# Up projection by seven block products per pair of inner tiles, with token-block sums made beside two plain pairs

## Chip, cores and metric

One core of one Trainium2 chip runs the whole layer. The metric is the device time of one execution in microseconds, median of several runs; the profile is one execution taken by the hardware profiler. Its span is the time from the first to the last instruction.

## What is computed

A decoder layer with 1024 tokens, width 1024 and 4096 inner channels, float32. The part that matters here is the feed-forward block at its end:

```python
x = x + jnp.concatenate([attn, conv], axis=-1) @ w_out[l]
h = rmsnorm(x, norm_ffn_g[l])
x = x + jnp.square(jax.nn.relu(h @ w_ffn_up[l])) @ w_ffn_down[l]
return rmsnorm(x, norm_final_g)
```

`h @ w_ffn_up` is 1024x1024 by 1024x4096, `... @ w_ffn_down` 1024x4096 by 4096x1024.

## The kernel before

Every float32 product is made of three reduced-precision matmuls: `split` (lines 54 to 56) makes a rounded high part on ScalarE and the remainder on VectorE or GpSimd (POOL), and `mm3` (lines 58 to 61) issues high x high, high x low and low x high into one PSUM bank.

The stages that the change and the prediction speak of, in order:

- **Output projection, convolution half, and the second norm** (lines 842 to 849). For each of 8 token tiles t, `conv_proj` makes 2 x 12 matmuls (tile `oc`) that VectorE adds to the residual `x2[t]`; `norm_rows` squares the row sum on ScalarE (line 116), takes the root on POOL (lines 82, 83) and scales on VectorE (line 145, tile `n_xn`, two buffers); `norm_cols` transposes on TensorE (line 151) and splits the result into `h2h`, `h2l`, which hold the normed tokens as [channel, token], one tile for each half of 512 tokens.
- **Up projection** (lines 871 to 894, 957 to 965), 16 pairs of inner tiles of 128 channels. `load_up` loads one pair of 1 MB a pair ahead and splits it. `up` makes four results of 128 channels by 512 tokens, each 8 x 3 matmuls: 96 matmuls a pair. ScalarE makes the relu (line 880), VectorE the product with it (line 881), then four sums (lines 889 to 892), and SP stores seven tiles of 256 KB to DRAM (`hid`). Those sums are what the down projection needs.
- **Down projection** (lines 897 to 1026). It already works by seven block products for eight, in 7 groups of 7 steps of 24 matmuls; an eighth group is plain. `prep` splits the operands two steps ahead, three buffers of `hi` and `lo`; `load_group` loads the next group; `sums` makes the weight differences on POOL. Of the seven sums of results, three lie in `xe` and four in the residual tiles `x2a`, to which VectorE adds (line 993). Tokens 0 to 511 and 512 to 1023 are the two token blocks; even and odd inner tiles, and the two halves of the output width, are the other blocks.
- **The end** (lines 1028 to 1057): the eighth group, the residual, the last norm and the store.

The order on each engine, the DMA queue SP among them, is set at build time by a scheduler with a timing model of its own (line 1085); each engine then runs its instructions strictly in that order, waiting on semaphores. A pool opened where another was released waits only for the tiles whose place it takes (`reuse_waits="tile"`). DMAs are all issued by SP; a DMA also waits for the landing of the one eight places before it.

Of the kernel before, what the change touches and what calls it, by code (L numbers as in the profile page):

```python
# [33 lines left out]
def body(tc, x, norm_mix_g, w_in, b_forget, conv_dw_w, conv_dw_b, conv_ln_g, conv_ln_b,  # L34
# [830 lines left out]
    def raw4(name):  # L865
        return rp.tile([P, 2, HN], F32, tag="raw4", name=name, bufs=11)
# [4 lines left out]
    def up(p, w):  # L871
        q = [raw4(f"q{p}{e}") for e in range(2)]
        for e in range(2):
            sl = slice(e * P, (e + 1) * P)
            for hf in range(2):
                ps = ps_two(f"up{p}{e}{hf}")[:, 0, :]
                for k in range(KT):
                    mm3(ps, w[0][:, k, sl], w[1][:, k, sl], h2h[hf][:, k, :], h2l[hf][:, k, :], k == 0, k == KT - 1)
                r = rp.tile([P, HN], F32, tag="r", name=f"r{p}{e}{hf}", bufs=2)
                A.activation(r, ps, AF.Relu)  # L880
                V.tensor_tensor(q[e][:, hf, :], ps, r, op=ALU.mult)  # L881
        a11, a21, a12, a22 = q[0][:, 0, :], q[0][:, 1, :], q[1][:, 0, :], q[1][:, 1, :]
        if p >= NPAIR - 2:
            for i, a in ((1, a11), (2, a12), (0, a21), (4, a22)):
                SP.dma_start(hid[i][p if i else p - NPAIR + 2], a)
            return
        s12, s34 = raw4(f"s12{p}"), raw4(f"s34{p}")
        s1, s2, s3, s4 = s12[:, 0, :], s12[:, 1, :], s34[:, 0, :], s34[:, 1, :]
        V.tensor_tensor(s1, a21, a22, op=ALU.add)
        V.tensor_tensor(s2, s1, a11, op=ALU.subtract)  # L890
        V.tensor_tensor(s3, a11, a21, op=ALU.subtract)
        V.tensor_tensor(s4, a12, s2, op=ALU.subtract)
        for i, a in ((1, a11), (2, a12), (4, a22), (5, s1), (6, s2), (7, s3), (3, s4)):
            SP.dma_start(hid[i][p], a)
# [9 lines left out]
    def wtile(g, name, dt=F32):  # L904
        if g == 0:
# [183 lines left out]
```

## Time and profile before

| what | before |
|---|---|
| median of 3 runs (lowest to highest) | 1196.79 us (1196.76 to 1197.3) |
| the profiled execution's own time | 1197.22 us |
| its span | 1195.2 us |
| granted TensorE clock, mean over the span | 0.995 |
| TensorE (PE) busy | 1158.0 us, 97% |
| VectorE (DVE) busy | 770.7 us, 64% |
| ScalarE (ACT) busy | 442.2 us, 37% |
| POOL busy | 330.0 us, 28% |
| DMA | 145.63 MB, mean 122 GB/s |

PE is the matrix engine, PEld its weight loads, which run beside it. Busy time is the union of an engine's instructions; L59 is line 59 of the kernel. An idle time is followed by what ended it in brackets. Consecutive matmuls overlap, so their spacing is read from start times, not from their durations.

### The profile page before, as it was taken

Reading aid. Unit: us, or ns where it says so; the run is one execution under the profiler, and the core shown is the slowest. Engines: PE = TensorE matmul, PEld = TensorE weight load, DVE = VectorE, ACT = ScalarE, POOL = GpSimd, SP = SyncE. Lnnn points to the kernel's source line nnn. Section 1 sums busy time; section 2 is a strip of 40 time slices with the busy share of each in tenths; the row PEclk is TensorE's granted clock in tenths of the full one; section 3 lists DMA queues with packets and bytes.
Section 4 is the critical chain, followed back from the end, with each engine's and each line's share of the span. In section 5 each row is a group of like instructions: output and inputs, shape, how many; then the busy total and the mean of one; then the engine's idle time right before and its main releaser. Section 6 shows DMA issues by size and latency. Waiting matters only on the chain.

```text
span 1195.2 us, 14915 instructions
## 1 busy us (share of the span) xinstructions
PE 1158.0 (97%) x5623; PEld 948.2 (79%) x5623; DVE 770.7 (64%) x1026; ACT 442.2 (37%) x691; POOL 330.0 (28%) x272
## 2 busy tenths in 40 slices
PE   6999999989999999979999999999999999999997
PEld 6899888767677688868888888888888888888876
DVE  5399999568888764552332423423268888878994
ACT  6322452147888841331211212111235343433422
POOL 7113255037788610100000000000163334443011
PEclk9999999999999999989999999999999999999999
DMA  8021045774232253023343443532495554444003
GB/s 267 13 60 49 23 122 126 205 192 123 72 116 62 84 179 91 1 80 103 118 167 106 138 144 107 172 111 104 159 347 189 168 164 137 136 154 141 1 12 129
DMA packets 92912, 145.63 MB, mean 122 GB/s; under 512 B 7896, under 2 KB 43048, under 8 KB 92840
## 3 DMA queue, kind: packets, MB, share of 16 engines
q1 hardware_dynamic: 92840, 144.68, 38.4%
q8 instruction: 44, 0.72, 0.2%
q14 instruction: 28, 0.23, 0.1%
HBM read 104.18 MB, written 40.40 MB: 121 GB/s over the span
## 4 chain that ended last, share of the span: by engine, by line
PE 86%; DVE 6%; issue 3%; ACT 2%; POOL 2%; DMA 1%; SPq 0%; DVEq 0%; POOLq 0%; ACTq 0%
PE up L60 10%; PE up L59 10%; PE up L61 10%; PE dn L61 7%; PE dn L59 7%; PE dn L60 7%; PE qk L59 2%; PE qk L60 2%; PE qk L61 2%; PE g L269 2%; PE v L61 1%; PE v L60 1%; PE v L59 1%; PE oc L59 1%; PE oc L60 1%
## 5 line engine op out<-in xcount | busy, mean ns | idle before, releaser
L881 DVE TENSOR_TENSOR q<-up,r 128x512 f32<-128x512 f32 x64 | 44.1, 689 | 161.4 <-ACT r L880 161.4
L292 DVE SCALAR_TENSOR_TENSOR conv<-u,par,conv 128x1024 f32<-128x1024 f32 x108 | 133.6, 1279 | 1.7 <-ACT conv L287 1.3
L880 ACT ACTIVATE r<-up 128x512 f32<-128x512 f32 x64 | 37.9, 593 | 216.3 <-PE up L61 216.3
L56 POOL TENSOR_TENSOR d01lo<-b,d01hi 128x1024 fp32r<-128x1024 f32 x1 | 2.4, 2392 | 326.6 <-ACT d01hi L55 326.6
L993 DVE TENSOR_TENSOR x<-dn,x 128x1024 f32<-128x1024 f32 x56 | 67.9, 1218 | 25.1 <-PE dn L61 25.0
L56 POOL TENSOR_TENSOR pl<-pt,ph 128x512 fp32r<-128x512 f32 (+3 forms) x71 | 74.7, 1067 | 26.2 <-ACT ph L55 22.4
L613 ACT ACTIVATE pt<-sT,ctok 128x512 f32<-128x512 f32 (+1 forms) x96 | 54.4, 585 | 11.6 <-PE sT L611 5.1
L453 DVE CUSTOM_DVE_ANT_0 mj<-s,ck 128x512 bf16<-128x512 f32 (+2 forms) x64 | 37.4, 584 | 19.5 <-PE s L447 13.5
L55 ACT ACTIVATE ph<-pt 128x512 fp32r<-128x512 f32 (+1 forms) x96 | 48.7, 530 | 0.6
L993 DVE TENSOR_TENSOR xe<-dn,xe 128x1024 f32<-128x1024 f32 x36 | 42.8, 1212 | 4.0 <-PE dn L61 4.0
L59 PE MATMUL qk<-hTh,wh_qk 128*128 128x512 f32 x96 | 39.0, 406 | 0.0
L60 PE MATMUL qk<-hTl,wh_qk 128*128 128x512 f32 x96 | 37.9, 395 | 0.0
L445 PE MATMUL s<-ks,q 128*128 128x512 f32 (+2 forms) x96 | 36.8, 390 | 1.0 <-DVE m L453 0.9
L61 PE MATMUL qk<-hTh,wl_qk 128*128 128x512 f32 x96 | 37.8, 394 | 0.0
L633 PE MATMUL av<-pl,v 128*65 128x512 f32 (+1 forms) x96 | 32.7, 341 | 3.9 <-POOL pl L56 2.3
L61 PE MATMUL v<-wh_v,hTl 128*128 128x260 f32 x128 | 36.2, 282 | 0.0
L60 PE MATMUL v<-wl_v,hTh 128*128 128x260 f32 x128 | 36.1, 282 | 0.0
L59 PE MATMUL v<-wh_v,hTh 128*128 128x260 f32 x128 | 36.0, 281 | 0.0
L631 PE MATMUL av<-ph,v 128*65 128x512 f32 (+1 forms) x96 | 35.5, 370 | 0.2 <-ACT ph L55 0.2
L608 PE MATMUL sT<-q,ks 128*128 128x512 f32 (+1 forms) x96 | 34.1, 355 | 0.1
L609 PE MATMUL sT<-qx,kx 66*128 66x512 f32 (+3 forms) x96 | 33.7, 351 | 0.0
L82 POOL TENSOR_SCALAR rs_tmp<-n_ss 128x1 f32<-128x1 f32 x16 | 6.6, 414 | 96.5 <-ACT n_xn L116 80.6
(926 smaller groups left out, 3692.2 us busy)
## 6 DMA issues: line engine op xcount, KB each, us to landing
h<-hid SPq DMA_DIRECT2D x53, 512.0 KB
b<-in_w_ffn_down SPq DMA_DIRECT2D x32, 512.0 KB
hid<-s SPq DMA_DIRECT2D x56, 256.0 KB
hid<-q SPq DMA_DIRECT2D x50, 256.0 KB
xp<-in_x SPq DMA_DIRECT2D x8, 512.0 KB
qstack<-qk SPq DMA_DIRECT2D x32, 128.0 KB
kstack<-qk SPq DMA_DIRECT2D x32, 128.0 KB
ks<-kstack SPq DMA_DIRECT2D x8, 512.0 KB
```

Of the source, the lines that this page charges most:

```text
L55: A.activation(hi, src, AF.Copy)
L56: eng.tensor_tensor(lo, src, f32(hi), op=ALU.subtract)
L59: T.matmul(ps, sh, mh, start=first, stop=False)
L60: T.matmul(ps, sh, ml, start=False, stop=False)
L61: T.matmul(ps, sl, mh, start=False, stop=last)
L292: V.scalar_tensor_tensor(dst, u[:, k:k + S], tap_w(c, k), cell[0], op0=ALU.mult, op1=ALU.add)
L445: T.matmul(ps[:, :w], d["q2"][:, i * P:(i + 1) * P], d["ks"][:, b0:b1], start=True, stop=b1 < n)
L453: V.tensor_tensor_reduce(junk[:, :w], ps[:, :w], d["ck"][:, b0:b1], op0=ALU.subtract, op1=ALU.max, scale=1.0, scalar=d.pop("m0") if b0 els ...
L613: A.activation(pt[:, :w], ps[:, :w], AF.Exp, bias=ctok[:, h * NT + kt:h * NT + kt + 1])
L880: A.activation(r, ps, AF.Relu)
L881: V.tensor_tensor(q[e][:, hf, :], ps, r, op=ALU.mult)
L993: V.tensor_tensor(a, ps, a, op=ALU.add)
```

## The change

In 14 of 16 pairs (pairs 2 to 15) the four results of a pair come from seven block products of 4 x 3 matmuls each, 84 matmuls in place of 96. The blocks are the two halves of the 1024 input channels, the two inner tiles of the pair, and the two token blocks. For this

- each pair's weights are loaded as four blocks of 256 KB, four sums or differences are made of them on POOL, and seven blocks (in place of eight) are split;
- of the tokens, four sums or differences of blocks (`mov[5]`, `mov[6]`, `mov[4]` and `mov[7]`) are made once, beside pairs 0 and 1, which stay plain. Their unsplit source is a float32 copy of the transposed normed tokens that `norm_cols2` writes to DRAM (`hraw`), tile by tile, and that is read back;
- after the products, results are combined: two ScalarE copies, one POOL add, six VectorE operations that read PSUM, and the square of the relu as one more VectorE operation on each of four results;
- for room, the residual goes to DRAM (`x2d`) and comes back at the start of the down projection into tiles that the up projection uses meanwhile; `raw4` has 8 buffers for 11 and its pool opens in the middle of the last pair, when products 1, 5 and 6 of it are made; the raw weights have 3 buffers for 2;
- the first two results of pair 0, on the first token block, are made ahead of the last tile's norm.

The core of the diff:

```diff
+    def norm_cols2(t):
...
+        split(h2h[hf][:, :, c:c + P], h2l[hf][:, :, c:c + P], pt.rearrange("p (k n) -> p k n", k=KT))
+        A.activation(xn, pt, AF.Copy)
+        SP.dma_start(hraw[:, :, t * P:(t + 1) * P].rearrange("k p n -> p k n"), xn.rearrange("p (k n) -> p k n", k=KT))
+    for t in range(NT):
+        for hf in range(2):
+            conv_proj(hf, t)
+        SP.dma_start(x2d[t], x2[t])
+        xns[t] = norm_rows(x2[t], gffn, pn, f"n2_{t}")
         if t >= 1:
-            norm_cols(xns.pop(t - 1), t - 1, h2h, h2l, f"n2_{t - 1}")
+            norm_cols2(t - 1)
...
+    def load_up7(p):
...
+        for dst, k0, e in ((g[2][:, 0], 0, 1), (g[2][:, 1], 4, 1), (g[0][:, 0], 0, 0), (g[1][:, 1], 4, 0)):
+            SP.dma_start(dst, w_up_k[:, k0:k0 + 4, c0 + e * P:c0 + (e + 1) * P])
+        G.tensor_tensor(g[0][:, 1], g[2][:, 0], g[2][:, 1], op=ALU.add)
+        G.tensor_tensor(g[1][:, 0], g[0][:, 1], g[0][:, 0], op=ALU.subtract)
+        G.tensor_tensor(g[2][:, 0], g[0][:, 0], g[2][:, 0], op=ALU.subtract)
+        split(ah[:, 0:2], al[:, 0:2], g[0])
+        split(ah[:, 2:4], al[:, 2:4], g[1])
+        G.tensor_tensor(g[1][:, 1], g[1][:, 1], g[1][:, 0], op=ALU.subtract)
+        split(bh[:, 0], bl[:, 0], g[1][:, 1])
+        split(bh[:, 1:3], bl[:, 1:3], g[2])
...
+    def make_moving(k):
+        b11, b12, b22, b21 = [load_hraw(f"b{r}{c}_{k}", 4 * r + k, c) for r, c in ((0, 0), (0, 1), (1, 1), (1, 0))]
+        G.tensor_tensor(b11, b12, b11, op=ALU.subtract)
+        split(*mov[5][k], b11)
+        G.tensor_tensor(b22, b22, b11, op=ALU.subtract)
+        split(*mov[6][k], b22)
+        G.tensor_tensor(b21, b21, b22, op=ALU.subtract)
+        split(*mov[4][k], b21)
+    def make_t3(k):
+        b12, b22 = load_hraw(f"c12_{k}", k, 1), load_hraw(f"c22_{k}", 4 + k, 1)
+        G.tensor_tensor(b12, b22, b12, op=ALU.subtract)
+        split(*mov[7][k], b12)
...
+    def up7(p, w, mid=None):
...
+        def relu2(dst, ps, other):
+            V.tensor_tensor(dst, ps, other, op=ALU.add)
+            V.scalar_tensor_tensor(dst, dst, 0.0, dst, op0=ALU.max, op1=ALU.mult)
+        A.activation(s1, prod(p, w, 1), AF.Copy)
+        A.activation(s5, prod(p, w, 5), AF.Copy)
+        V.tensor_tensor(u2, prod(p, w, 6), s1, op=ALU.add)
+        if mid is not None:
+            mid()
+        G.tensor_tensor(s5, s5, u2, op=ALU.add)
+        relu2(q[:, 0, 0, :], prod(p, w, 2), s1)
+        relu2(q[:, 0, 1, :], prod(p, w, 3), s5)
+        p7 = prod(p, w, 7)
+        V.tensor_tensor(u2, p7, u2, op=ALU.add)
+        relu2(q[:, 1, 1, :], p7, s5)
+        sums_up(p, False)
+        relu2(q[:, 1, 0, :], prod(p, w, 4), u2)
+        sums_up(p, True)
...
+    for e in range(2):
+        up_half(0, uws[0], e, 0, ps_mm(f"up0{e}0"))
+    norm_cols2(NT - 1)
...
+            load_h(0, SEQ0[3])
+            reload_x2(0)
+            reload_x2(1)
+            load_h(0, SEQ0[4])
+            reload_x2(2)
+            reload_x2(3)
+            for i in SEQ0[5:]:
                 load_h(0, i)
             sums(0)
-            V.tensor_tensor(acc_of[3], acc_of[3], acc_of[5], op=ALU.subtract)
             continue
         g, i = steps[n]
+        if n == 3:
+            for h in range(2):
+                V.tensor_tensor(acc_of(3, h), acc_of(3, h), acc_of(5, h), op=ALU.subtract)
```

What the scheduler makes of it, at three places. **ScalarE at the end of the second norm**, tiles 5 to 7 (`n_7_t` the transposed tile 7, `n_7_xn` its normed rows; `work_q<-up` the relu of pair 0). Before:

```order
L55 ACTIVATE h2h_5103<-n_4_t 128x8x128
L116 ACTIVATE n_6_xn,n_6_ss<-x_4822 128x1024
L55 ACTIVATE up2h<-up2r_5517 128x1024
L55 ACTIVATE up2h<-up2r_5521 128x1024
L55 ACTIVATE h2h_5103<-n_5_t 128x8x128
L55 ACTIVATE h2h_5103<-n_6_t 128x8x128
L55 ACTIVATE up4h<-up4r_5654 128x1024
L116 ACTIVATE n_7_xn,n_7_ss<-x_4822 128x1024
L55 ACTIVATE up4h<-up4r_5658 128x1024
L55 ACTIVATE h2h_5103<-n_7_t 128x8x128
```

With the change:

```order
L55 ACTIVATE uhi2a<-ur_5711 128x1024
L854 ACTIVATE n_4_xn<-n_4_t 128x1024
L55 ACTIVATE uhi2a<-ur_5712 128x1024
L55 ACTIVATE h2h_5106<-n_5_t 128x8x128
L889 ACTIVATE work_q<-up_5523 128x512
L116 ACTIVATE n_6_xn,n_6_ss<-x_4825 128x1024
L854 ACTIVATE n_5_xn<-n_5_t 128x1024
L889 ACTIVATE work_q<-up_5550 128x512
L116 ACTIVATE n_7_xn,n_7_ss<-x_4825 128x1024
L55 ACTIVATE h2h_5106<-n_6_t 128x8x128
L854 ACTIVATE n_6_xn<-n_6_t 128x1024
L55 ACTIVATE h2h_5106<-n_7_t 128x8x128
```

The square of tile 6 (L116) moved behind a copy of tile 4 into its old buffer (L854), the split of tile 6 behind the square of tile 7; on PE the transposes of tiles 6 and 7 stand after all 48 early matmuls of pair 0.

**ScalarE at the start of the down projection** (`d05hi` is the split of step 5 of group 0: `h` its tokens, `t` or `b` its weights). Before:

```order
L991 ACTIVATE xe<-dn_7755 128x1024
L991 ACTIVATE xe<-dn_7769 128x1024
L55 ACTIVATE d05hi<-h_0_7713 128x1024
L55 ACTIVATE d05hi<-t_0_7721 128x1024
L55 ACTIVATE d06hi<-h_0_7715 128x1024
L55 ACTIVATE d06hi<-t_0_7722 128x1024
L55 ACTIVATE d07hi<-h_0_7717 128x1024
```

With the change:

```order
L1136 ACTIVATE xe<-dn_7945 128x1024
L1136 ACTIVATE xe<-dn_7959 128x1024
L55 ACTIVATE d05hi<-h_0_7892 128x1024
L55 ACTIVATE d06hi<-h_0_7900 128x1024
L55 ACTIVATE d07hi<-h_0_7908 128x1024
L55 ACTIVATE d05hi<-t_0_7912 128x1024
L55 ACTIVATE d06hi<-t_0_7913 128x1024
```

The weight half of step 5 moved behind the token halves of steps 6 and 7; there are three `hi` buffers, so `d07hi` takes the place of `d03hi`.

**POOL beside pairs 0 and 1** (`b_0` to `b_3` and `c_0` to `c_3`: token blocks read back; `ur`: weights of pair 3). Before, POOL has nothing between the last norm and the first split of the down projection. With the change:

```order
L965 TENSOR_TENSOR b_2_5734<-b_2_5736,b_2_5734 128x512
L930 TENSOR_TENSOR ur_5887<-ur_5889 128x512
L967 TENSOR_TENSOR b_2_5738<-b_2_5738,b_2_5734 128x512
L931 TENSOR_TENSOR ur_5888<-ur_5887 128x512
L932 TENSOR_TENSOR ur_5889<-ur_5887,ur_5889 128x512
L965 TENSOR_TENSOR b_3_5751<-b_3_5753,b_3_5751 128x512
L969 TENSOR_TENSOR b_2_5740<-b_2_5740,b_2_5738 128x512
L967 TENSOR_TENSOR b_3_5755<-b_3_5755,b_3_5751 128x512
L969 TENSOR_TENSOR b_3_5757<-b_3_5757,b_3_5755 128x512
L974 TENSOR_TENSOR c_0_5910<-c_0_5912,c_0_5910 128x512
```

Ahead of these stand six more for `b_0` and `b_1`, behind them three for `c_1` to `c_3`: 19 new operations between the norm and the end of pair 1.

## Rows read from the trace of the kernel before

**Rows 1.** Busy time of the page, engines' share of the span.

```profile
PE 1158.0 (97%) x5623; PEld 948.2 (79%) x5623; DVE 770.7 (64%) x1026; ACT 442.2 (37%) x691; POOL 330.0 (28%) x272
```

**Rows 2.** Windows: stretch, length, busy time (count) by engine, PEclk, DMA share, GB/s.

```profile
510.00:520.00 10.00, 6.49 (x37) 5.28 (x35) 8.00 (x8) 6.06 (x7) 0.74 (x2) 1.00 0.33 102
520.00:526.00 6.00, 1.50 (x7) 1.53 (x8) 4.77 (x4) 2.08 (x4) 1.73 (x2) 0.55 0.30 92
548.00:570.00 22.00, 22.00 (x99) 18.22 (x98) 7.53 (x10) 4.29 (x6) 0.00 (x0) 1.00 0.39 133
885.00:890.00 5.00, 5.00 (x24) 4.14 (x23) 5.00 (x3) 2.01 (x2) 4.92 (x3) 1.00 1.05 401
1100.00:1150.00 50.00, 49.45 (x215) 39.64 (x214) 48.39 (x42) 18.32 (x19) 4.79 (x2) 1.00 0.01 4
```

**Rows 3.** Instructions of tiles up and dn: ns min/median/max, first and last start.

```profile
L59 PE MATMUL up<-h2h,up0h x32: 387/389/776, 526.1 to 547.9; 128*128 128x512 f32 x32
L59 PEld LDWEIGHTS up<-h2h,up2h x32: 187/188/188, 548.4 to 569.4; 128*128 128x128 f32 x32
L59 PE MATMUL up<-h2h,up2h x32: 389/389/390, 548.6 to 569.7; 128*128 128x512 f32 x32
L59 PE MATMUL up<-h2h,up4h x32: 389/389/390, 570.3 to 591.4; 128*128 128x512 f32 x32
L59 PE MATMUL dn<-d01hi x8: 389/389/390, 875.0 to 879.7; 128*128 128x512 f32 x8
```

**Rows 4.** PE in order of time, last two transposes of the norm.

```profile
515.46 1.03 PE L151 MATMUL n_t<-ident,n_xn 128*128 128x128 f32 x8
524.50 1.94 PE L151 MATMUL n_t<-ident,n_xn 128*128 128x128 f32 x8 [8.01 <-DVE n_xn L145]
```

**Rows 5.** ScalarE, POOL and VectorE in order of time, one tile's norm.

```profile
484.55 1.06 ACT L116 ACTIVATE n_xn<-x 128x1024 f32<-128x1024 f32 x1 [1.89 <-DVE x L815]
487.17 1.03 ACT L55 ACTIVATE h2h<-n_t 128x1024 fp32r<-128x1024 f32 x1 [1.47 <-PE n_t L151]
...
485.78 0.19 POOL L82 TENSOR_SCALAR rs_tmp<-n_ss 128x1 f32<-128x1 f32 x1 [5.96 <-ACT n_xn L116]
486.06 0.55 POOL L83 TENSOR_TENSOR n_rs<-rs_tmp,mhalf 128x1 f32<-128x1 f32 x1
...
486.90 1.28 DVE L145 SCALAR_TENSOR_TENSOR n_xn<-x,n_rs,gffn 128x1024 f32<-128x1024 f32 x1
488.22 1.22 DVE L56 TENSOR_TENSOR h2l<-n_t,h2h 128x1024 fp32r<-128x1024 f32 x1
```

**Rows 6.** SP and ScalarE in order of time: one 512 KB load and its reader.

```profile
851.35 0.46 SPq L920 DMA_DIRECT2D h<-hid  x1
...
855.34 1.06 ACT L55 ACTIVATE d02hi<-h 128x1024 fp32r<-128x1024 f32 x1 [0.37 <-DMA h<-hid]
```

**Rows 7.** Groups by form: count, busy us, mean ns, idle before.

```profile
L881 DVE TENSOR_TENSOR q<-up,r 128x512 f32<-128x512 f32 x64 | 44.1, 689 | 161.4 <-ACT r L880 161.4
L889 DVE TENSOR_TENSOR s<-q,q 128x512 f32<-128x512 f32 x14 | 9.7, 692 | 0.5
L56 DVE TENSOR_TENSOR up8l<-up8r,up8h 128x1024 fp32r<-128x1024 f32 x2 | 2.4, 1222 | 5.0 <-ACT up8h L55 5.0
L880 ACT ACTIVATE r<-up 128x512 f32<-128x512 f32 x64 | 37.9, 593 | 216.3 <-PE up L61 216.3
L55 ACT ACTIVATE up6h<-up6r 128x1024 fp32r<-128x1024 f32 x2 | 2.0, 1052 | 4.6 <-PE up L60 4.6
L936 POOL TENSOR_TENSOR t<-b,b 128x1024 f32<-128x1024 f32 x7 | 17.9, 2552 | 32.5 <-issue 12.9 <-DMA b<-in_w_ffn_down 5.1 <-DVE d57lo L56 3.1
```

**Rows 8.** VectorE, then POOL, in order of time, a steady group of the down projection.

```profile
1034.09 2.97 DVE L56 TENSOR_TENSOR d45lo<-h,d45hi 128x1024 fp32r<-128x1024 f32 x1
1036.99 1.21 DVE L56 TENSOR_TENSOR d45lo<-t,d45hi 128x1024 fp32r<-128x1024 f32 x1
1038.12 2.34 DVE L993 TENSOR_TENSOR xe<-dn,xe 128x1024 f32<-128x1024 f32 x2
...
1033.58 2.41 POOL L938 TENSOR_TENSOR b<-b,b 128x1024 f32<-128x1024 f32 x1
1038.28 2.42 POOL L937 TENSOR_TENSOR t<-b,t 128x1024 f32<-128x1024 f32 x1 [2.30 <-DVE d45lo L56]
```

More of the change, by code (lines that the diff above doesn't have):

```diff
@@ L781, in body @@
     x2p = pool("x2p", "left")
-    x2a = x2p.tile([P, NT, D], F32, name="x2")
-    x2 = [x2a[:, t, :] for t in range(NT)]
+    x2t = [x2p.tile([P, 2, D], F32, tag=f"x{h}", name=f"x2{h}", bufs=1) for h in range(NT // 2)]
+    x2 = [x2t[t // 2][:, t % 2, :] for t in range(NT)]
     for t in range(NT):
@@ L792, in load_w2 @@
         for k in range(0, shape[1], half):
-            raw = wgt.tile([P, half, shape[2]], F32, tag="raw", name=f"{name}r{k}", bufs=2)
+            raw = wgt.tile([P, half, shape[2]], F32, tag="raw", name=f"{name}r{k}", bufs=3)
             SP.dma_start(raw, src[:, k:k + half, :])
@@ L865, in raw4 @@
     def raw4(name):
[L866 removed]
+        return rps[0].tile([P, 2, HN], F32, tag="raw4", name=name, bufs=8)
     def load_up(j):
         return load_w2(w_up_k[:, :, j * P:(j + 2) * P], f"up{j}", [P, KT, 2 * P])
[L871 to L894 removed]
@@ new lines, in body, with open_work, up_half @@
+    work = {}
+    def open_work():
+        work["q"] = x2p.tile([P, 2, 2, HN], F32, tag="x0", name="work_q", bufs=1)
+        work["s"] = x2p.tile([P, 4, HN], F32, tag="x1", name="work_s", bufs=1)
+    def up_half(p, w, e, hf, ps):
+        sl = slice(e * P, (e + 1) * P)
+        for k in range(KT):
+            mm3(ps, w[0][:, k, sl], w[1][:, k, sl], h2h[hf][:, k, :], h2l[hf][:, k, :], k == 0, k == KT - 1)
+        q = work["q"][:, e, hf, :]
+        A.activation(q, ps, AF.Relu)
+        V.tensor_tensor(q, ps, q, op=ALU.mult)
@@ new lines, in store, with sums_up @@
+    def store(p, i, a):
+        SP.dma_start(hid[i][p if i else p - NPAIR + 2], a)
+    def sums_up(p, last):
+        q, sm = work["q"], work["s"]
+        a11, a21, a12, a22 = q[:, 0, 0, :], q[:, 0, 1, :], q[:, 1, 0, :], q[:, 1, 1, :]
+        s1, s2, s3, s4 = [sm[:, i, :] for i in range(4)]
+        plain = p >= NPAIR - 2
+        if not last:
+            store(p, 1, a11)
+            store(p, 4, a22)
+            if plain:
+                store(p, 0, a21)
+                return
+            V.tensor_tensor(s1, a21, a22, op=ALU.add)
+            V.tensor_tensor(s2, s1, a11, op=ALU.subtract)
+            V.tensor_tensor(s3, a11, a21, op=ALU.subtract)
+            for i, a in ((5, s1), (6, s2), (7, s3)):
+                store(p, i, a)
+        else:
+            store(p, 2, a12)
+            if not plain:
+                V.tensor_tensor(s4, a12, s2, op=ALU.subtract)
+                store(p, 3, s4)
@@ L904, in wtile @@
     def wtile(g, name, dt=F32):
[L905 removed]
+        if "wr" not in pools_d:
             return raw4(f"{name}_{g}")
```

116 lines of the change are left out of this document (87 added, 29 removed).

## The prediction

> **What bounds the kernel now.** First the page's busy line: PE is busy 97% of the span, its weight loads 79%, VectorE 64%, ScalarE 37%, POOL 28% [rows 1]; the reader should see that nothing but PE can be the bound on average. Then the windows, since an average says nothing of a stage: in a pair of the up projection PE is busy 22.00 of 22.00 us at clock 1.00, VectorE 7.53, ScalarE 4.29, POOL not at all, and the DMA engines 39% [rows 2]. Then PE's rows by tile, for the price of a matmul: in steady state 32 matmuls of one kind follow each weight tile, and the next tile starts 21.7 us later (548.6 to 570.3); a pair is three such sets, so I need the spacing itself: from the up projection's start at 526.1 to the down projection's at 875.0 stand 16 x 96 = 1536 matmuls, 0.227 us each; and one pair, 548.6 to 570.3, is 96 in 21.7 us, **0.226 us a matmul**. The weight load takes 0.188 and fits inside it [rows 3]. The first pair, 526.1 to 548.6, takes 22.5, so 0.8 us more: its first matmuls run at up to 776 ns, half speed, after an idle stretch in which the mean clock was 0.55 [rows 2, 3]. Last, PE's own order at the only large gap ahead of the tail: between the transposes of the last two tiles of the second norm PE waits 8.01 us for VectorE's scaled rows [rows 4].
>
> **The change, part by part.**
>
> *Removed matmuls.* 14 pairs lose 12 of 96: 168 x 0.226 = **-38.0 us**, all of it on PE's path.
>
> *A pair on the other engines.* A new pair lasts 84 x 0.226 = 18.97 us on PE. By form [rows 7], VectorE has six operations that read PSUM (0.69 each, 4.1 in all), four relu squares and four sums (8 x 0.69 = 5.5), and of the splits three of 1024 elements and one of 512 (3 x 1.22 + 0.69 = 4.3): 13.9 us. ScalarE has two copies (0.59 each) and splits of 3 x 1.05 + about 0.55: 4.9 us. POOL has four weight sums and one addition of 512 elements; only 1024 is in the trace, 2.55 us, so I take half, 1.25: 6.25 us. Each alone fits in 18.97. They touch, though: beside a POOL operation that started at 1033.58 and took 2.41, a VectorE operation with two SBUF inputs took 2.97 in place of 1.21 and ended 1.07 after POOL's end, while one that reads PSUM took its usual 2.34 for two [rows 8]. So the two engines' SBUF operations queue: 5.5 + 4.3 + 6.25 = 16.0 us, which still fits in 18.97; only if the PSUM reads can never lie beside them does it come to 20.1 and miss. Four PSUM buffers hold 4 x 12 matmuls, 10.8 us, and weights are split a pair ahead, so I expect the delays to be taken up. DMA: 1 MB in and 1.75 MB out, as before, some 7 us at the 401 GB/s that the trace shows where the DMA engines are full [rows 2]. **0**, from 0 to +19 (14 x 1.1 by the lower bound of all operations serial, plus 4 for waits in order).
>
> The Trainium skill, page "SBUF — State Buffer", section "SBUF: two separate sides", says that the port pair of VectorE and GpSimd is an exclusive lock, held for a whole instruction by whichever starts first, and taken by a VectorE operation with two SBUF inputs against a GpSimd operation that reads SBUF. The rows on 1034.09 agree, with 2.97 us against 1.21. By that rule this change, which puts POOL into a stage where it did nothing, could cost more than its busy times tell; rival C below is that mechanism.
>
> *The second norm.* 48 matmuls of pair 0 (10.85 us) are now ahead of the last tile and would fill the gap of 8.0. But a tile's chain now passes a store: there are two `n_xn` buffers, the raw copy of tile t is written into one of them, and the square of tile t+2 waits for its store. Chain for two tiles [rows 5]: transposes 1.03, split 1.03 and 1.22, copy 1.03, store of 512 KB, square 1.06, root 0.19 + 0.55, scale 1.28; the store I price as the load of 512 KB, from issue at 851.35 to its reader's start at 855.34, 4.0 us [rows 6]. With about 1 us of hops this is 12.4 us against PE's 2 x (24 x 0.226 + 1.03) = 12.9, so it is hidden until the last two tiles. There ScalarE has weight splits of pair 1 queued ahead (some 4 us, and waits for their loads). Walked through: PE's early matmuls end at 515.46 + 10.85 = 526.3; scaled rows of tile 6 come at about 529.4, of tile 7 at 535.5; transposes, split and remainder of tile 7 end at 540.0, and the slow restart costs 0.8 as before: 540.8. Before, the same point (48 matmuls into pair 0) was at 526.1 + 10.85 + 0.8 = 537.75. **+3.0**, from -8 (gap filled) to +10 (each 0.5 us on a store moves it by 2 to 2.5).
>
> *POOL beside pairs 0 and 1.* 19 operations x 1.25 = 23.8 us that start at R + 8.3 (R: PE's resumption; copy 1.0, store 4.0, load of 256 KB 3.3, which is 4.0 less 256 KB at 401 GB/s), with some 0.4 of port wait each: end at R + 40. Behind the last stand, in ScalarE's order, its split, a split of weights of pair 3, a relu and the copy of pair 2's product 1: R + 43.6. PE wants that copy by R + 41.2. **+2.5**, from 0 to +8.
>
> *Start of the down projection.* The high half of step 5's weights now stands on ScalarE behind step 7's token half, which waits for the third buffer, that is for the end of step 3: 3 x 24 x 0.226 = 16.3 us after the first matmul. Only then come two ScalarE splits (1.05 each) and three VectorE operations of 1.2 in order, one of which may meet a POOL operation (up to 2.4 more). PE has two matmuls to issue meanwhile: about 5 us idle. Its next products then wait 1.4 for VectorE's addition from PSUM, and the clock restarts slowly, 0.8. Before, PE had no wait here. **+7.0**, from +3 to +12.
>
> *Elsewhere* nothing: the down projection in steady state and the tail keep their order, where VectorE is busy 48.39 of 50 us beside PE's 49.45 [rows 2]; some 18 MB of extra DRAM traffic lie where the DMA share is 0.3 to 0.4.
>
> **Sum:** -38.0 + 3.0 + 2.5 + 7.0 = **-25.5**. The profiled execution took 1197.22 us, 0.43 above the median of 1196.79; so it would come to 1171.7, and the median to **1171.3**.
>
> **Rivals.**
>
> *A, the covers hold.* ScalarE's queue at the two transitions has slack that I have counted as wait, for instance because stores land sooner than 4.0 us and the down projection's tiles come earlier. Then only the matmuls count: 1196.8 - 38.0 = 1158.8; with the gap at the norm filled as well, 1152. For it: PE's busy share leaves everything else idle half the time. Against: ScalarE's order at both places, which stands. Chance 0.15.
>
> *B, VectorE and POOL set the pair.* All their work in a row, 20.1 us: 14 x (21.7 - 20.1) = 22.4 gained, less the 12.5 of the transitions: about 1187. For it: one thread of waits goes back and forth between them (`s5` on POOL needs `u2` from VectorE, the third product's addition needs `s5`). Against: PSUM reads run beside POOL undisturbed [rows 8]. Chance 0.13.
>
> *C, slower.* Each POOL operation shuts VectorE out for its whole length, PSUM reads queued behind the blocked one included, and in each pair VectorE stands still once more while POOL makes `s5`, which itself needs `u2` just written: 1.25 for the addition and 0.69 for the operation behind it, some 2.0. That is 13.9 + 6.25 + 2.0 = 22.15 us a pair against 21.7 before: 14 x 0.45 + 12.5 = 18.8 lost, about 1215.6. It decides from 21.7 - 12.5/14 = 20.8 us a pair on. For it: in the one row, VectorE got nothing done until POOL ended (1.07 us after, of the 1.21 that it takes). Against: it needs every POOL operation to meet a VectorE one, and no buffer to help. Chance 0.06.
>
> **How the numbers follow.** A difference of 0.2% (2.4 us) is about what a measurement of this kernel can tell. My forecast has 0.66, with a range of its own from 1162 to 1180 (its three positive terms at their lower and upper ends, not all at once). To hold 8 in 10 the range takes in the near edge of A and all of B: 1160 to 1188. Faster by over 0.2%: forecast, A, B and the little between, 0.91; slower 0.06; within 0.2% the 0.03 that lie between B and C.
>
> **What would show it.** PE's first matmuls of two neighbouring pairs 18.97 us apart in pairs 4 to 14, with no PE wait inside, and VectorE busy 14 to 16 us of it, show the main term; 20 or more, with VectorE or POOL as releaser of PE, shows B or C, and VectorE operations of two SBUF inputs well above 0.69 beside POOL show the lock. At the norm: a PE wait of about 8 to 10 us ahead of the second half of pair 0, released by VectorE, with stores of `hraw` as what the squares waited for. At pair 2: a short wait of product 2 for ScalarE's copy. At step 5 of the down projection's first group: 5 us of PE idle, released by VectorE's remainder, ScalarE waiting for PE ahead of `d07hi`. The prediction is wrong if the pair takes longer than 20 us, or if PE waits inside the down projection's later groups, where I count nothing.

## The result and the profile after

The changed kernel takes 1182.65 us (median of 4 runs, 1181.25 to 1183.88), the kernel before in the same series 1197.05 us: a ratio of 0.988, 95% interval 0.9865 to 0.9895. It is 14.4 us faster; forecast were 25.5, and the range, 1160 to 1188, holds the time. The profiled execution has a span of 1180.2 us, 15.0 less than before. Busy time of the page, as in [rows 1]:

```profile
PE 1128.8 (96%) x5455; PEld 918.7 (78%) x5455; DVE 905.4 (77%) x1155; ACT 466.2 (40%) x715; POOL 461.1 (39%) x358
```

PE lost 29 us of work, VectorE gained 135 and POOL 131. Where the span changed is read from the first starts of tiles on PE, as in [rows 3]. The changed kernel (count; ns min/median/max, first and last start; `oc` is the convolution half of the output projection, `u<-t1s` product 5 of a pair, of pairs 2, 3 and 15 here):

```profile
L59 PE MATMUL oc<-wo10h,cmh x32: 393/396/397, 464.4 to 509.0; 128*128 128x512 f32 x32
L59 PE MATMUL up<-h2h,up2h x32: 389/389/389, 548.8 to 569.9; 128*128 128x512 f32 x32
L59 PE MATMUL u<-h2h,uhi2a x8: 389/508/796, 570.6 to 589.5; 128*128 128x512 f32 x8
L59 PE MATMUL u<-t1s,uhi2a x4: 394/396/399, 573.3 to 575.4; 128*128 128x512 f32 x4
L59 PE MATMUL u<-t1s,uhi3a x4: 394/396/399, 601.7 to 603.8; 128*128 128x512 f32 x4
L59 PE MATMUL u<-t1s,uhi15a x4: 394/396/399, 832.6 to 834.7; 128*128 128x512 f32 x4
L59 PE MATMUL dn<-d01hi x8: 389/389/389, 849.1 to 853.9; 128*128 128x512 f32 x8
L59 PE MATMUL dn<-d11hi x8: 389/389/389, 898.2 to 903.0; 128*128 128x512 f32 x8
```

The kernel before, the convolution half and the second group of the down projection:

```profile
L59 PE MATMUL oc<-wo10h,cmh x32: 395/397/398, 465.6 to 511.1; 128*128 128x512 f32 x32
L59 PE MATMUL dn<-d11hi x8: 389/389/390, 913.1 to 917.8; 128*128 128x512 f32 x8
```

From these rows and [rows 3]:

| stretch | before, us | after, us | difference | forecast |
|---|---|---|---|---|
| start to the convolution half | 465.6 | 464.4 | -1.2 | 0 |
| convolution half and norm, to pair 1 | 83.0 | 84.4 | +1.4 | +3.0 |
| pair 1 | 21.7 | 21.8 | +0.1 | 0 |
| pairs 2 to 15 | 304.7 | 278.5 | -26.2 | -38.0 + 2.5 |
| first group of the down projection, to the second's first matmul | 38.1 | 49.1 | +11.0 | +7.0 |
| the rest | 282.1 | 282.0 | -0.1 | 0 |

The first line is no work of the change: in the other traces of kernels with this stage as it is here, the convolution half starts at 463.8 to 466.8. The second line is steady: in e1, e2, e4 to e7, e10 and e11, which leave it as it is, it is 84.1 to 85.1 us.

The line of pairs 2 to 15 has three parts. Pairs 3 to 15 repeat every (832.6 - 601.7) / 12 = 19.24 us. Pair 2 takes 601.7 - 573.3 = 28.4, which is 9.2 more. And 14 x (19.24 - 84 x 0.2267) = 2.8, where 0.2267 is the spacing before, 304.7 / 1344. Removed are 168 x 0.2267 = 38.1: -38.1 + 9.2 + 2.8 = -26.1.

Windows of the changed kernel, columns as in [rows 2]: pair 1, the restart of PE in pair 2, and a later pair:

```profile
548.80:570.50 21.70, 21.70 (x97) 17.98 (x96) 21.67 (x17) 8.44 (x14) 20.09 (x12) 1.00 0.62 201
585.00:591.00 6.00, 5.55 (x13) 4.40 (x14) 4.75 (x7) 1.28 (x3) 2.28 (x2) 0.51 0.77 262
601.00:620.00 19.00, 19.00 (x84) 15.59 (x83) 15.85 (x19) 4.55 (x7) 7.63 (x5) 1.00 0.45 151
```

In a later pair PE never waits and VectorE has 3.15 us to spare. Beside pair 1 VectorE is full and POOL nearly so. After its wait in pair 2 PE has a granted clock of 0.51, half speed, from 585 to 591. PE in order of time, every wait of it between the norm and the down projection's second group:

```profile
526.92 1.07 PE L851 MATMUL n_t<-ident,n_xn 128*128 128x128 f32 x8 [1.57 <-DVE n_xn L145]
532.29 1.94 PE L851 MATMUL n_t<-ident,n_xn 128*128 128x128 f32 x8 [4.30 <-DVE n_xn L145]
535.34 0.79 PE L59 MATMUL up<-h2h,up0h 128*128 128x512 f32 x1 [1.11 <-ACT h2h L55]
536.60 0.79 PE L60 MATMUL up<-h2l,up0h 128*128 128x512 f32 x1 [0.47 <-DVE h2l L56]
585.45 0.80 PE L59 MATMUL u<-h2h,uhi2a 128*128 128x512 f32 x1 [6.37 <-ACT us L991]
867.67 0.73 PE L59 MATMUL dn<-d05hi 128*128 128x512 f32 x2 [2.09 <-ACT d05hi L55]
872.81 0.80 PE L60 MATMUL dn<-d05lo,d05hi 128*128 128x512 f32 x1 [4.40 <-DVE d05lo L56]
881.74 0.47 PE L59 MATMUL dn<-d06hi 128*128 128x512 f32 x1 [1.41 <-DVE xr L1138]
```

Three places, then, each with its own question: pair 2, the start of the down projection, and the norm, where 48 early matmuls could have filled the gap of [rows 4] and nothing was gained: PE waits 7.45 us there in four pieces.

**Pair 2.** VectorE, then POOL, beside pair 1, in order of time:

```profile
561.13 1.78 DVE L906 TENSOR_TENSOR work_s<-work_q 128x512 f32<-128x512 f32 x1
562.83 1.77 DVE L56 TENSOR_TENSOR t2s<-b,t2s 128x512 fp32r<-128x512 f32 x1
...
562.32 1.74 POOL L932 TENSOR_TENSOR ur<-ur,ur 128x512 f32<-128x512 f32 x1
564.01 1.74 POOL L965 TENSOR_TENSOR b<-b,b 128x512 f32<-128x512 f32 x1
...
573.62 1.35 POOL L974 TENSOR_TENSOR c<-c,c 128x512 f32<-128x512 f32 x1 [2.76 <-DMA c<-hraw]
580.61 1.26 POOL L974 TENSOR_TENSOR c<-c,c 128x512 f32<-128x512 f32 x1 [0.66 <-DMA c<-hraw]
```

The two engines take turns: each gets one operation done every 1.70 us, where alone VectorE's lasts 0.69 [rows 7] and POOL's, by the last row, 1.26. The Trainium skill, page "SBUF — State Buffer", section "SBUF: two separate sides", says that a VectorE operation with two SBUF inputs and a GpSimd operation that reads SBUF lock each other out for whole instructions. The trace agrees, with 1.77 us against 0.69. POOL's string ends at 581.87, and ScalarE comes to the copy that PE waits for only behind it:

```profile
581.90 0.63 ACT L55 ACTIVATE h2h<-c 128x512 fp32r<-128x512 f32 x1 [1.29 <-POOL c L974]
582.44 1.99 ACT L55 ACTIVATE uhi3a<-ur 128x1024 fp32r<-128x1024 f32 x2
584.33 0.57 ACT L889 ACTIVATE work_q<-up 128x512 f32<-128x512 f32 x1
584.81 0.58 ACT L991 ACTIVATE us<-u 128x512 f32<-128x512 f32 x1
```

**The down projection's start.** VectorE in order of time, and the POOL operation beside it:

```profile
866.76 1.58 DVE L56 TENSOR_TENSOR d07lo<-h,d07hi 128x1024 fp32r<-128x1024 f32 x1
868.26 3.36 DVE L1160 TENSOR_TENSOR xr<-xr,xr 128x1024 f32<-128x1024 f32 x1
871.54 1.21 DVE L56 TENSOR_TENSOR d05lo<-t,d05hi 128x1024 fp32r<-128x1024 f32 x1
...
867.21 3.33 POOL L1048 TENSOR_TENSOR b<-b,b 128x1024 f32<-128x1024 f32 x1
```

The subtraction of the residual (L1160) lasts 3.36 us for 1.21 beside POOL, and d05lo, for which PE waits, stands behind it.

### The profile page after: what moved, and what is told of

Same layout as the page of the kernel before. It is cut to its first block, busy times and chain, and to the rows that moved or that the text cites. A ratio compares the mean times of both kernels' runs of the same rounds, so it can differ in the third digit from the quotient of the medians.

```text
span 1180.2 us, 15131 instructions
## 1 busy us (share of the span) xinstructions
PE 1128.8 (96%) x5455; PEld 918.7 (78%) x5455; DVE 905.4 (77%) x1155; ACT 466.2 (40%) x715; POOL 461.1 (39%) x358
## 4 chain that ended last, share of the span: by engine, by line
PE 56%; DVE 7%; ACT 4%; issue 3%; DMA 3%; POOL 2%; SPq 0%; DVEq 0%; POOLq 0%; ACTq 0%
PE u L59 7%; PE u L60 7%; PE u L61 7%; PE dn L60 7%; PE dn L61 7%; PE dn L59 7%; DMA hraw<-n_xn 2%; PE op L59 1%; PE op L61 1%; PE op L60 1%; DVE xr L1138 1%; PE fin L59 1%; PE fin L61 1%; PE fin L60 1%; PE s L445 1%
## 5 line engine op out<-in xcount | busy, mean ns | idle before, releaser
L1138 DVE TENSOR_TENSOR xr<-dn,xr 128x1024 f32<-128x1024 f32 x56 | 68.0, 1219 | 35.9 <-PE dn L61 35.8
L935 POOL TENSOR_TENSOR ur<-ur 128x512 f32<-128x512 f32 x14 | 22.7, 1620 | 93.4 <-DVE ulo6a L56 7.4
L989 DVE SCALAR_TENSOR_TENSOR work_q<-work_q 128x512 f32<-128x512 f32 x56 | 52.7, 942 | 1.0
L988 DVE TENSOR_TENSOR work_q<-u,us 128x512 f32<-128x512 f32 x42 | 28.6, 681 | 26.9 <-PE u L61 26.9
L60 PE MATMUL qk<-hTl,wh_qk 128*128 128x512 f32 x96 | 37.9, 395 | 0.0
L631 PE MATMUL av<-ph,v 128*65 128x512 f32 (+1 forms) x96 | 35.3, 368 | 0.1
L930 POOL TENSOR_TENSOR ur<-ur 128x512 f32<-128x512 f32 x14 | 24.5, 1750 | 25.3 <-DVE up2l L56 2.5
```

The source lines that it names most:

```text
L60: T.matmul(ps, sh, ml, start=False, stop=False)
L631: T.matmul(av[:DH + 1, o0:], v1, ph[:, :w], start=kt == ORDER[hf][0], stop=False)
L989: V.scalar_tensor_tensor(dst, dst, 0.0, dst, op0=ALU.max, op1=ALU.mult)
L1138: V.tensor_tensor(a, ps, a, op=ALU.add)
```

## The experiments

Theory Q (order of queues): PE waits because ScalarE and VectorE work strictly in order, and work that isn't ready stands ahead of work that is. Its rivals name a resource instead: the transfers and results of the residual's reload (D, R), POOL's string and the turns with VectorE (P, L), the stores at the norm (S). All edits but those named are on the changed kernel, whose own stage lengths stand above.

### e1: weight block b12 loaded early

```diff
 def begin_down():
...
             load_b(0, nm)
             load_h(0, i)
+        load_b(0, "12")
...
-            load_b(0, "12")
             load_h(0, SEQ0[3])
```

> Edit: the load of the weight block b12 of the down projection's first group stands with the first six loads, in the middle of the last pair, in place of behind the second step's splits; nothing else. In the trace of the changed kernel the first group's 7 steps take 11.1 us longer than before (875.0 to 907.6 before, 849.1 to 892.8 now). Theory Q (order of queues): POOL's first weight difference waits for b12 until 862.3, so that step 5's weights come late and behind step 7's tokens on ScalarE, and VectorE's subtraction of the residual meets a POOL operation (3.36 us for 1.2). With b12 early the weight half of step 5 stands ahead of step 6's token half again: at least 8 of the 11.1 us come back, device time about 1173 to 1175, PE waits under 1.5 us in the first group. Rival D (transfer): the DMA engines are full there (388 to 408 GB/s) since 4 MB of residual are read back, and whatever loads first makes another tile late: 0 to 3 us come back, and PE waits for the token half of a step or for the residual instead.

Measured: 1183.1 us (1178.7 to 1183.85), ratio 0.9874 (0.9854 to 0.9894); the profiled execution is the one of 1178.7, so stage lengths decide, not its span. ScalarE's order is as forecast, and step 5 starts without a wait (863.2, straight behind step 3). But the first group takes 894.9 - 846.8 = 48.1 us, 1.0 less only, because PE now waits at step 6, and twice more, 1.11 us each, at step 7:

```profile
872.83 0.47 PE L59 MATMUL dn<-d06hi 128*128 128x512 f32 x1 [3.98 <-DVE xr L1139]
878.37 0.50 PE L59 MATMUL dn<-d06hi 128*128 128x512 f32 x1 [1.11 <-ACT xe L1137]
```

VectorE in the same kernel:

```profile
868.15 3.39 DVE L56 TENSOR_TENSOR d07lo<-b,d07hi 128x1024 fp32r<-128x1024 f32 x1
871.47 1.21 DVE L1139 TENSOR_TENSOR xr<-dn,xr 128x1024 f32<-128x1024 f32 x1
...
883.42 1.22 DVE L56 TENSOR_TENSOR d11lo<-h,d11hi 128x1024 fp32r<-128x1024 f32 x1 [5.26 <-ACT d11hi L55]
884.56 2.35 DVE L1139 TENSOR_TENSOR xr<-dn,xr 128x1024 f32<-128x1024 f32 x2
```

Results of steps 2 and 3 for the first token half, finished by 863, are added only at 884.56: their residual tiles come into the place of `work_q`, which is stored last. Until then they hold two of the four PSUM buffers. Theory Q's forecast, 8 us back, falls here; D stands, in the form that the runs e5 to e7 try. Order is not out altogether: in the trace's DMA records the packets of the residual's last two loads end at 877.2, and from 878.16 to 883.42 VectorE stood for a split of the next group that is ahead of the two additions in its order.

### e2: the t3 sums written behind products 1, 5 and 6 of pair 2

```diff
-            if p == NPL:
-                for k in range(4):
-                    make_t3(k)
-            up7(p, uws.pop(p), begin_down if p == NPAIR - 1 else None)
+            up7(p, uws.pop(p), begin_down if p == NPAIR - 1 else make_t3s if p == NPL else None)
```

> Edit: the four differences t3 (mov[7]) and their splits are written behind products 1, 5 and 6 of pair 2, not ahead of them; ScalarE's order then has the two copies of pair 2 and the weight splits of pair 3 ahead of the t3 splits. In the trace of the changed kernel pair 2 takes 28.4 us against 19.24 of a later one (PE idle 6.37 ahead of product 2's matmuls, released by ScalarE's copy, then some 6 us at half clock): 9.2 lost. Theory Q: the copies wait only because they stand behind the t3 splits in ScalarE's order, which wait for POOL; now at least 7 of the 9.2 us come back, device time 1174 to 1176. Rival P (POOL's string): pairs 0 and 1 leave POOL and VectorE full (20.1 and 21.7 of 21.7 us in pair 1), so that the work is late whatever its order: PE waits instead at product 7 of pair 2, or for the weights of pair 3, and 0 to 4 us come back.

Measured: 1179.89 us (1178.02 to 1182.2), ratio 0.9856 (0.9839 to 0.9873). From product 5 to product 5, pair 2 takes 595.0 - 573.0 = 22.0 us and pair 3 617.9 - 595.0 = 22.9: of 9.2 us too many 6.4 are left (2.8 and 3.6). PE waits 2.91 us for ScalarE's t3 split, then 1.29 for VectorE. The order was worth 2.8 by these two traces (in e1 and e4 to e7, which leave pair 2 as it is, it takes 26.7 to 28.8 us, so 1 to 3); the rest only moved on, as rival P says.

### e3: three plain pairs

```diff
-    NPL = 2
+    NPL = 3
...
-            for k in range(2 * p, 2 * p + 2):
+            for k in ((0, 1), (2,), (3,))[p]:
```

> Edit: three plain pairs for two, with two of the four sets of token-block sums beside pair 0 and one beside each of pairs 1 and 2; 13 pairs of seven products are left, which costs 12 x 0.227 = 2.7 us of matmuls. Rival P: POOL's string of 19 operations gets 65 us in place of 43, the stall of 9.2 us at the first pair of seven products goes: -9.2 + 2.7 = -6.5, device time about 1176, though the t3 splits still stand ahead of the copies. Theory Q: as long as the copies stand behind the t3 splits, which can start only when pair 2's last matmuls have read the tiles that they overwrite, a wait stays, of some 3 to 5 us with the slow restart of PE behind it: -2 or so, about 1180.

Measured: 1177.08 us (1174.89 to 1180.62), ratio 0.9832 (0.9807 to 0.9857). Pair 3, now the first of seven products, takes 617.2 - 598.0 = 19.2 us without a stall, though the t3 splits still stand ahead of the copies. One wait of 1.45 us is left at the start of pair 2. Rival P again.

### e10: no differences on POOL

```diff
-        G.tensor_tensor(b11, b12, b11, op=ALU.subtract)
         split(*mov[5][k], b11)
-        G.tensor_tensor(b22, b22, b11, op=ALU.subtract)
         split(*mov[6][k], b22)
-        G.tensor_tensor(b21, b21, b22, op=ALU.subtract)
         split(*mov[4][k], b21)
```

> Edit on the changed kernel: beside pairs 0 and 1 the 12 differences of token blocks on POOL are left out; the blocks themselves are split in their place, so that products 4, 5 and 6 have wrong operands; loads, splits and everything else stay. Theory P (POOL's string, made longer by VectorE beside it): POOL is done early, VectorE's operations with two SBUF inputs beside pair 1 go back from up to 1.78 us to 0.69, pair 2's stall of 6.4 us ahead of product 2 falls under 1.5 us, and pair 2 takes under 21 us (28.4 in the changed kernel). Rival O (order and loads): the t3 splits still stand ahead of the copies, wait for the last matmuls of pair 1 and for loads that wait for buffers and for the queue: a stall of 4 us or more stays.

Measured: one run, 1173.9 us. Pair 2 has no wait at all:

```profile
L59 PE MATMUL u<-t1s,uhi2a x4: 394/396/399, 574.0 to 576.1; 128*128 128x512 f32 x4
L59 PE MATMUL u<-t1s,uhi3a x4: 394/396/399, 593.3 to 595.4; 128*128 128x512 f32 x4
```

19.3 us. ScalarE's order is the same, so the order alone makes no stall: POOL's string makes it. VectorE's operations beside pair 1 are partly back to 0.68 us, partly still 1.77, beside the weight sums and t3 differences that were left on POOL.

### e5: the residual not read back

```diff
-            SP.dma_start(x2[-1], x2d[2 * h + e])
...
-            if g == 0 and i in (1, 6, 7):
+            if g == 0:
                 A.activation(a, ps, AF.Copy)
...
-        if n == 3:
-            for h in range(2):
-                V.tensor_tensor(acc_of(3, h), acc_of(3, h), acc_of(5, h), op=ALU.subtract)
```

> Edit on the changed kernel: the residual isn't read back (4 MB less) and the first results of block products 2 to 5 are copied by ScalarE in place of added by VectorE, so the output lacks the residual; the two subtractions of residual halves are gone as well. First group of the down projection (7 steps, 38.1 us without a wait): 43.7 us from its first matmul to that of its seventh step in the changed kernel, 32.6 before. Theory R (reload): the 4 MB that share full DMA engines, and the results that wait in PSUM for them, are the cause: 32.6 to 35 us, b12 lands early enough without being moved. Rival O (order of ScalarE and POOL): b12 is still loaded behind the others and the two weight halves still stand behind token halves: 39 us or more.

Measured: one run, 1175.43 us. To the seventh step 886.2 - 850.9 = 35.3 us, for the whole group 40.7 (49.1 with the reload): 8.4 of 11.0 come back with b12 where it was. One PE wait is left:

```profile
870.19 0.50 PE L60 MATMUL dn<-d05lo,d05hi 128*128 128x512 f32 x1 [2.32 <-DVE d05lo L56]
```

That d05lo took 3.40 us beside a POOL operation of 3.35. So theory R for the greater part, and the turns with POOL for the rest. But the run changed more than the loads: VectorE's subtraction ahead of d05lo is gone, and ScalarE has another order, in which the weight half of step 5 is ahead of step 7's token half:

```profile
864.78 1.06 ACT L55 ACTIVATE d05hi<-t 128x1024 fp32r<-128x1024 f32 x1
...
868.49 1.07 ACT L55 ACTIVATE d07hi<-h 128x1024 fp32r<-128x1024 f32 x1
```

### e6 and e7: the residual's tiles exchanged, and another order of steps

e6 is e1 and

```diff
-        x2t.append(x2p.tile([P, 2, D], F32, tag=f"x{h}", name=f"xr{h}", bufs=1))
+        x2t.append(x2p.tile([P, 2, D], F32, tag=f"x{(h + 2) % 4}", name=f"xr{h}", bufs=1))
```

> Edit: b12 early (as in the first run) and the residual tiles exchange places: the first two, which steps 2 and 3 need, come back into the place of t4s, the last two into that of work_q and work_s, which is stored last. Then the results of steps 2 and 3 needn't wait for the last stores of the up projection. Theory R: results held in PSUM for the late residual (two of four buffers) are what made PE wait at step 6 with b12 early; now PE's waits in the first group fall from 7.3 us (4.0 + 3.3) to under 4, the group from 42.7 to 37 or less. Rival L (lock): VectorE's operations of 2.3 to 3.4 us beside POOL's three weight differences of the next group make the wait; they stay, and the group takes 41 us or more.

Measured: 1177.0 us (1175.57 to 1178.94), ratio 0.9836 (0.9817 to 0.9855). The group takes 43.3 us, to its seventh step 37.9; one wait of 3.42 us for VectorE's addition is left. That lies between the two forecasts and decides nothing by itself. e7 adds

```diff
-    SEQ0 = (1, 2, 3, 5, 6, 7, 4)
+    SEQ0 = (1, 2, 3, 6, 7, 5, 4)
...
-        if n == 3:
+        if n == SEQ0.index(5):
```

> Edit: as the run before, and the first group's steps go 1, 2, 3, 6, 7, 5, 4 in place of 1, 2, 3, 5, 6, 7, 4: steps 6 and 7 need no residual (their results are copied), so that the residual's last half is needed 10.9 us later. Theory R: PE's waits in the first group under 1 us, 33 to 34 us for its first six steps, some 9 us less than in the changed kernel, device time about 1173. Rival L: waits of 4 us or more stay, for VectorE's operations held by POOL.

Measured: 1175.51 us (1174.07 to 1176.61), ratio 0.9822 (0.9807 to 0.9836). The group takes 892.2 - 851.9 = 40.3 us, 8.8 less than in the changed kernel. The one wait left is longer than theory R allowed:

```profile
881.45 0.50 PE L60 MATMUL dn<-d05lo,d05hi 128*128 128x512 f32 x1 [1.75 <-DVE d05lo L56]
```

Its releaser took 3.40 us beside a POOL operation of 3.36. With the full computation this recovers what leaving the reload out did (40.7): with b12 early, it is the place and time of the reload that cost, not its 4 MB.

### e8: the raw copy written into the residual's tile

```diff
-        A.activation(xn, pt, AF.Copy)
+        A.activation(x2[t], pt, AF.Copy)
```

(and the store reads it from there.)

> Edit: the float32 copy of the transposed normed tokens is written into the tile of the residual, which is in DRAM by then, in place of the normed rows' buffer, so that the square of tile t+2 no longer waits for a store; the number of copies and stores is the same. In the changed kernel the scaled rows of tile 7 are ready 7.8 us later than before (532.3 for 524.5), which eats what 48 early matmuls gain. Theory S (store): the squares wait 13.3 us in all for stores; without them tile 7 is ready by 526 to 527, PE's wait of 4.3 us ahead of its transposes and of 1.6 ahead of tile 6's are gone, pair 1 begins about 5 us earlier (543 to 545 for 548.8). Rival A (ScalarE's queue): splits of weights of pairs 1 and 2 and the copies stand ahead of the last squares, each with its own wait for a load; tile 7 comes 1 to 2 us earlier at most and PE gains as much.

Measured: 1177.07 us (1176.91 to 1177.29), ratio 0.9836 (0.9821 to 0.985). Pair 1 begins at 542.2 for 548.8, so 6.6 us earlier, and the convolution half starts later, at 466.3: from there to pair 1 it is 75.9 us for 84.4, 8.5 less. The waits for scaled rows are gone; the first row is PE's next wait at the norm, the second the stall at pair 2, which grew from 6.37:

```profile
530.13 0.49 PE L59 MATMUL up<-h2h,up0h 128*128 128x512 f32 x1 [1.11 <-ACT h2h L55]
581.84 0.80 PE L59 MATMUL u<-h2h,uhi2a 128*128 128x512 f32 x1 [8.73 <-ACT us L991]
```

Theory S is right. In the changed kernel the stores of two raw copies on that chain take 3.97 and 3.20 us, and the squares of tiles 6 and 7 start behind them.

### e4 and e11: why products 5 and 6 are slower on PE

e4 takes `[:, 32:32 + CT * S]` of the places of t1s and t2s for `[:, :CT * S]`; e11 writes the copy of product 5 ahead of that of product 1.

> Edit: the tiles t1s and t2s (moving operands of products 5 and 6) start 32 elements (128 bytes) further into their place. In the trace of the changed kernel three matmuls take 0.703 us with these two as moving operand and 0.680 with h2h, h2l or t4s, 0.19 us a pair. Their place is 4128 elements (16512 bytes) for 4096, at the end of the memory, so that t2s begins 128 bytes, and t1s 256 bytes, off a multiple of 16384 from that end. Theory of the start address: with the shift t2s is aligned and falls to 0.680, t1s is 128 bytes off and stays at 0.70. Rival: it's something else about these tiles (who writes beside them): both stay at 0.703. Device time changes by 1.3 us or nothing.

> Edit on the changed kernel: product 5 is made ahead of product 1 in each pair, and so with t1s as moving operand first. In the changed kernel three matmuls take 0.703 us in products 5 and 6 (second and third of the pair, with t1s and t2s) and 0.680 in all others but the first of product 2. A shift by 128 bytes changed nothing. Theory of place: the slow reads belong to the tiles t1s and t2s; product 5 is slow as the first of the pair, product 1 is fast as the second. Theory of time: the second and third product of a pair lie beside something (splits, stores) that slows PE: product 1 is slow as the second, product 5 fast as the first.

Measured, one run each: 1180.94 and 1184.0 us. The shift changes nothing, four groups of three still take 2.80 to 2.81 us. e11, first matmul of each group:

```profile
715.49 0.40 PE L59 MATMUL u<-t1s,uhi9a 128*128 128x512 f32 x1
716.19 0.40 PE L59 MATMUL u<-t1s,uhi9a 128*128 128x512 f32 x1
...
718.29 0.40 PE L59 MATMUL u<-h2h,uhi9a 128*128 128x512 f32 x1
718.99 0.40 PE L59 MATMUL u<-h2h,uhi9a 128*128 128x512 f32 x1
719.68 0.39 PE L59 MATMUL u<-h2h,uhi9a 128*128 128x512 f32 x1
720.37 0.39 PE L59 MATMUL u<-h2h,uhi9a 128*128 128x512 f32 x1
```

A group with t1s takes 0.70 us as the pair's first product too, which speaks for the place; but product 1, with h2h, behind it takes 0.70, 0.69, 0.69 and 0.68, which the place alone doesn't explain. The start address is out as the cause; what it is stays open. It costs 0.2 us a pair, 2.8 in all.

### e9 and e12: the moves together

e9 has e7's edits, e8's and e3's.

> Edit: four moves together: b12 early, residual tiles' places exchanged and steps 1, 2, 3, 6, 7, 5, 4 (run e7: first group of the down projection 40.3 us from its first matmul to the next group's, 49.1 in the changed kernel); the raw copy into the residual's tile (e8: pair 1 begins 6.6 us earlier); three plain pairs (e3: the first pair of seven products without a stall, 12 matmuls more). If the three places are independent, each keeps what it gave alone: 1182.65 - 8.8 - 6.6 - (9.2 - 1.8 - 2.7 = 4.7) = 1162.5, range 1160 to 1166. Rival: what is gained at the norm is lost again at POOL's string, which starts only a little earlier (in e8 the stall of pair 2 grew by 1.4 to 2.3 us): 1167 to 1170.

Measured: 1161.46 us (1161.02 to 1163.61), ratio 0.9715 (0.9699 to 0.9731), inside its range. Pair 1 begins at 540.0, pair 3 has no stall (19.2 us), the first group takes 42.9 us, 2.6 more than in e7 (a wait of 2.30 us for d05lo again). The three places are nearly independent.

e12 has two plain pairs, e7's and e8's edits, and

```diff
 def make_moving(k):
...
-        G.tensor_tensor(b11, b12, b11, op=ALU.subtract)
+        V.tensor_tensor(b11, b12, b11, op=ALU.subtract)
...
```

(all four kinds of differences of token blocks.)

> Edit: run e9's moves at the norm and at the down projection, but two plain pairs as in the changed kernel (12 matmuls, 2.7 us, fewer than in e9), and the 16 differences of token blocks beside them on VectorE in place of POOL. In the changed kernel the two engines take turns beside pair 1: a VectorE operation of two SBUF inputs lasts 1.77 us for 0.69, a POOL one 1.74 for 1.26, one of each every 1.70. Theory L (the turns make the string long): on VectorE a difference costs 0.69 and holds nobody up; VectorE then has some 36 us of work beside pairs 0 and 1 (43 us), pair 2 has no stall over 2 us where e8, with the same norm, had 8.7, and the kernel takes 1158 to 1161. Rival N (too much work for the two pairs, wherever it lies; loads of hraw late): a stall of 4 us or more stays at pair 2, and the kernel takes 1163 or more.

Measured: 1160.3 us (median of 5, 1158.06 to 1163.64), ratio 0.9695 (0.9676 to 0.9715). Pair 2 takes 586.7 - 566.8 = 19.9 us, with one wait of 0.33 us. VectorE beside pair 1, and the window of pair 1:

```profile
557.12 0.68 DVE L914 TENSOR_TENSOR work_s<-work_q,work_s 128x512 f32<-128x512 f32 x1
557.72 0.68 DVE L967 TENSOR_TENSOR b<-b,b 128x512 f32<-128x512 f32 x1
```

```profile
542.40:564.10 21.70, 21.70 (x97) 17.99 (x96) 20.47 (x30) 9.14 (x16) 5.22 (x3) 1.00 0.81 253
```

VectorE does 30 operations in 20.47 us here; in the changed kernel 17 filled 21.67. Theory L is right: the difference on POOL cost VectorE more than making it itself. e12 and e9, of which e12 was to be 2.7 us faster for its matmuls, differ by 1.2 with overlapping intervals; both beat the two kernels of the comparison.

## Why the prediction was right in sign and short in size

The main term and the sign came as reasoned. That the range holds the time is partly luck: 1182.65 lies outside 1162 to 1180, the forecast's own range, and inside 1160 to 1188 only by the room left for rival B, whose mechanism did not come. Three terms were too small, by 6.7, 4.0 and 2.8 us, and one too large, by 1.6.

- **Removed matmuls, -38.0:** right, -38.1.
- **A pair on the other engines, 0:** right as to waits: 12 intervals of 19.24 us in pairs 3 to 15, VectorE at 15.85 of 19.0 (14 to 16 were named). The turns with POOL are there and are absorbed: by group, from 620 to 820 us, L989 has a mean of 907 ns and L908 of 1663, for the 0.69 of [rows 7]. Wrong by 0.2 us a pair: matmuls that read t1s and t2s are slower, which no row of before could show. Rivals B and C, 20 us and more a pair, did not come.
- **The second norm, +3.0:** measured +1.4, from the start of the convolution half. The mechanism was right (squares behind stores; e8 gave 8.5 us by removing it). PE's wait for the last tile was shorter than the 8 to 10 us named: 4.30, and 1.57 ahead of the tile before. The walk put the times too late: scaled rows of tile 7 were forecast for 535.5 and came at 532.1. Of these 3.4 us, 2.6 were there at tile 6 (526.8 for 529.4), 1.2 of them from the earlier start of the stage, and 0.8 are the last store (3.20 us for 4.0).
- **POOL beside pairs 0 and 1, +2.5:** measured +9.2, outside the term's own range (0 to +8); the term most mis-sized. With the rest as measured, the point called R in the working lies at 548.8 - 10.85 = 537.95. PE did want the copy by R + 41.1 (forecast R + 41.2), and ScalarE's own part took 3.5 us (3.6). But POOL ended at R + 43.9, not R + 40. The 19 operations took 30.3 us with the turns, as priced (19 x 1.65 = 31.4); what was left out is 7.2 us of waits between them, 5.8 of these for the loads of `c`. I priced the wait of each POOL operation, not that of VectorE, which was full (21.67 of 21.70) and so freed the buffers late for which the loads of `c` wait; POOL then stood 2.76 and 2.19 us for them. That VectorE's lateness is what holds those loads is argued from the windows; that the string and its turns make the stall is shown by e10, e3 and e12. The last 2.8 us are, nearly all, the slow clock, which had no place in this term.
- **Start of the down projection, +7.0:** measured +11.0. Who released PE was as forecast, down to VectorE's subtraction beside POOL. PE stood 7.9 us (about 5 + 1.4 forecast) and lost 3.1 more (0.8), most of it at half clock. But the step "only then come two ScalarE splits and three VectorE operations" is not the only cause: with b12 early it was gone, and the group kept 10.0 of its 11.0 us (e1). A second cause of nearly the same length stood beside it, the residual's reload, counted at nothing under "elsewhere". The loss went where the reload was taken out (8.4 us, e5) or out of the way (8.8, e7). In both runs the step was gone too, by another order in e5 and by the early b12 in e7, so what the step costs without the reload stays open.
- **Elsewhere, 0:** right but for that reload: -0.1 from the down projection's second group on. The -1.2 ahead of the convolution half is the spread of executions.

The slow clock was priced too low in both places, at nothing in the POOL term and at 0.8 us in the other. The 0.8 was read from the first pair before, whose restart had spent its first stretch in the transposes [rows 4] (1.94 us for 1.03). After 6.37 us of idleness 13 matmuls took 5.6 us (585.45 to 591.03), about twice their 2.9.

Rival A's number, 1158.8, was nearly reached in the end, by e12 with 1160.3, but only after three edits at the transitions: the covers did not hold by themselves.

## What to carry to other kernels

When work is taken off the bounding engine, price the transitions with both queues of a shared resource, not only the one whose operations are added: a 0.69 us operation moved from VectorE to POOL can cost VectorE 1.1. Before mending a wait by its releaser, ask what is late within the next few microseconds; in e1 the named wait went and nine tenths of the loss stayed. And where a buffer is parked and reloaded, give the first reload the place that comes free first.
